# Order of the value transposes, the modulation sums and the softmaxes in the attention stages of a decoder trunk

## The chip, the core and the metric

One NeuronCore of one Trainium2 chip runs the whole program. The metric is the device time of one execution in microseconds (us). Engines are named as in the profile: PE is TensorE's matmuls and PEld its weight loads, DVE is VectorE, ACT is ScalarE, POOL is GpSimd, and SP is the engine whose queue issues most DMAs.

## The reference

One layer for a sequence of 512 positions of 1024 channels, in float32:

```python
cs = silu(c)
mod = cs @ w_ada + b_ada                  # 6 rows of 1024: shift1, scale1, gate1, shift2, scale2, gate2
h = rmsnorm(x, norm1_g) * (1 + scale1) + shift1
qa, ka, va, qd, kd, vd, ga, gd = split(h @ w_in)
out_a = sliding_window_attention(qa, ka, va, sinks)   # 8 heads, 2 kv heads, window 128, ALiBi, sinks
out_d = diff_attention(qd, kd, vd, lam)               # 4 heads, two softmax maps each, causal, ALiBi, RMSNorm
merged = sigmoid(ga) * (out_a @ w_branch_swa) + sigmoid(gd) * (out_d @ w_branch_diff)
x = x + gate1 * (merged @ w_out)
h2 = rmsnorm(x, norm2_g) * (1 + scale2) + shift2
x = x + gate2 * conv_ffn(h2)              # 1024 -> 2 x 2816, causal conv of width 3, GELU, -> 1024
return rmsnorm(x, final_g)
```

## The kernel before, in words

**Arithmetic.** A float32 product is made of three matmuls: each operand is split into a rounded part (`_h`, or `hi`) and a remainder (`_l`, or `lo`), and `mm3` adds hi·hi, hi·lo and lo·hi. A split is one ACT cast and one DVE subtraction (`split`, lines 115 and 116; `evac`, lines 430 to 434, for results that leave PSUM). So each weight block and each evacuated result costs both engines an instruction, DVE behind ACT.

**Stages.** The first 60 us normalise x and make the projections of the sliding-window queries, keys and values (tiles a0 to a5). Then come the projections of the differential heads together with the sliding-window attention (60 to 125 us), then the gates and branches of the first mixer together with the differential attention (125 to 230 us), then the gates of the second mixer, the merge and the output projection (to some 366 us), and the MLP. The change lies between 60 and 230 us.

**Who sets the order.** From line 485 on, TensorE's order is written by hand (`manual_schedule` for it alone): it executes what the program traces, in that order. DVE, ACT, POOL and SP are ordered by a planner when the kernel is built, by priority, then by the place in the trace, and by when the planner expects an operand to be ready; once built, each engine's queue is in order. `tc.high_priority(offset=HP)` puts instructions ahead of others that are ready. `tc.issue_after(ins)` queues what its block traces on the engine of `ins`, and only on that engine, behind `ins`; no wait for its end is added.

**Steps of filling.** `fill(n)` emits n steps of projection work on TensorE. A step is three matmuls of 512 columns; eight steps make a 128-column projection. `units` lists the projections to come, `prefetch` loads and splits their weights up to two ahead. A counter `tick` counts the steps. Work given to `after(n, fn)` is traced n steps later. At every eighth step, from step 8 on, `fill` calls `next(ada)`.

**Modulation rows.** `ada_rows` (line 750) makes four of the six modulation rows in eight halves of 512 columns. A call loads two blocks of w_ada (an SP DMA into a tile ra, one of four "raw" slots that weights share) and adds them, times silu(c), to the running sum `arow` with two DVE multiplies (lines 762 and 764). Behind the fourth call of a half the next one splits the sum (`arh`, `arl`) and hands the last part to `after(ADA_LAG, ...)`, with a lag of one step: `ada_spread` (line 771) sums over the partitions with two matmuls against ones, ACT copies a row out, and POOL writes it to `mod_rows` in DRAM. Past step 20 the multiplies have half the softmaxes' priority offset. The sum has one buffer, so the next half's first multiply waits for that DMA.

**Sliding-window attention.** Four pairs of heads. For a pair, `swa_scores(i, n0)` computes the scores of two 128-query blocks, with DVE adding the distance and taking the maximum (line 563); `swa_softmax(i)` scales the maxima (574), lets ACT do the exponentials with sums (575, 578) and DVE normalise (582, 583, 586), for the two heads j in turn; `swa_transpose(i, j)` transposes the probabilities of one head in two blocks (tile tp, line 598) into "t" banks of PSUM, of which there are two, and evacuates them into pTh and pTl; `swa_values(i)` multiplies them with the values `va`. `turn_va` (line 448) makes `va` out of the projected vaT by four transposes (tile pva, a "t" bank too) and two `evac`s. `evac_q(3)` evacuates the queries of the last pair, which share a bank with `swa_values`' result.

**Differential attention.** For head h and query block n, s = 4h + n: `diff_scores`, `diff_softmax` (lines 686 to 701: scaled maxima, two exponentials, then reciprocal, product with lambda, scaling and the difference of the two maps), `diff_transpose` (tile td, line 709) and, once a head is complete, `diff_values`. Blocks n = 0 and n = 1 of a head have their scores made together, and their softmaxes are traced one behind the other.

Of the kernel before, what the change touches and what calls it, by code (L numbers as in the profile page):

```python
# [11 lines left out]
ALU = mybir.AluOpType  # L12
# [15 lines left out]
HP = 100000  # L28
ST = 6
ADA_LAG = 1  # L30
# [6 lines left out]
SWA_FILL = (2, 2, 5, 2, 2, 2, 2, 3)  # L37
# [16 lines left out]
def kernel(  # L54
# [22 lines left out]
    nc = tc.nc  # L77
# [168 lines left out]
    ac, mods, wts = {}, {}, {}  # L246
# [191 lines left out]
    def evac_q(i):  # L438
        evac(qa[:, i, 0], qa[:, i, 1], acc6[i], qsc[:, i : i + 1])
# [55 lines left out]
    def fill(n):  # L495
        for _ in range(n):
            if not current:
                prefetch()
                if loaded:
                    wts, run = loaded.pop(0)  # L500
                    current.append(run(wts))
                    if tick[0]:
                        prefetch()
            if tick[0] == 7:
                prefetch()
            if current:
                try:
                    next(current[0])
                except StopIteration:
                    current.clear()  # L510
            for e in list(later):
                e[0] -= 1
                if e[0] <= 0:
                    later.remove(e)
                    e[1]()
            tick[0] += 1
            if tick[0] >= ADA_START and tick[0] % ADA_EVERY == 0:
                next(ada, None)

    def after(n, fn):  # L520
        later.append([n, fn])
# [14 lines left out]
    def swa_scores(i, n0):  # L536
        if n0 == 0:
            c = pairs[i] = Pair()
            c.mx, c.nm, c.lsum, c.es = (
                ap.tile([P, 2, NT], F32, tag=t, bufs=2, name=f"{t}{i}") for t in ("mx", "nm", "lsum", "es")  # L540
            )
            c.sb = [ap.tile([P, 2, P], F32, tag="st0", bufs=2, name=f"st{i}_0")]
            c.sb += [ap.tile([P, 2, 256], F32, tag="st", bufs=ST, name=f"st{i}_{n}") for n in range(1, NT)]
            c.pT = []
        c = pairs[i]
        sps = [sbank(f"sw{i}_{n0}_{j}", (P, 2, 256)) for j in range(2)]
        for n in (n0, n0 + 1):
            w = P if n == 0 else 2 * P
            k0 = max(0, n - 1) * P
            qs, ks = slice(n * P, (n + 1) * P), slice(k0, k0 + w)  # L550
            mm3_rows([
                (
                    sps[j][:, n - n0, :w],
                    [qa[64 * j : 64 * j + 64, i, b, qs] for b in range(2)],
                    [ka[64 * j : 64 * j + 64, b, ks] for b in range(2)],
                )
                for j in range(2)
            ])
        for n in (n0, n0 + 1):
            w = P if n == 0 else 2 * P  # L560
            for j in range(2):
                with tc.high_priority(offset=HP):
                    c.last = nc.vector.tensor_tensor_reduce(
                        c.sb[n][:, j, :w], sps[j][:, n - n0, :w], dsw[:, 256 - w : 256], 1.0, -3e38, ALU.add, ALU.max,
                        c.mx[:, j, n : n + 1],
                    )

    def swa_softmax(i):
        with tc.high_priority(offset=HP):
            c = pairs[i]  # L570
            for j in range(2):
                h = i + 4 * j
                slope = 2.0 ** -(h + 1)
                nc.vector.tensor_scalar(c.nm[:, j], c.mx[:, j], -slope, nsink[:, h : h + 1], ALU.mult, ALU.min)
                nc.scalar.activation(c.es[:, j], c.nm[:, j], AF.Exp, bias=sink[:, h : h + 1])
                for n in range(NT):
                    w = P if n == 0 else 2 * P
                    nc.scalar.activation(
                        c.sb[n][:, j, :w], c.sb[n][:, j, :w], AF.Exp, bias=c.nm[:, j, n : n + 1], scale=slope,
                        accum_out=c.lsum[:, j, n : n + 1],  # L580
                    )
                nc.vector.tensor_add(c.lsum[:, j], c.lsum[:, j], c.es[:, j])
                nc.vector.reciprocal(c.lsum[:, j], c.lsum[:, j])
                for n in range(NT):
                    w = P if n == 0 else 2 * P
                    nc.vector.tensor_scalar_mul(c.sb[n][:, j, :w], c.sb[n][:, j, :w], c.lsum[:, j, n : n + 1])

    def swa_transpose(i, j):
        c = pairs[i]
# [94 lines left out]
            scored[s] = mx, pm  # L684

    def diff_softmax(s):
        with tc.high_priority(offset=HP):
            h, n = divmod(s, NT)
            slope = 2.0 ** (-2 * (h + 1))
            mx, pm = scored[s]  # L690
            lsum = ap.tile([P, 2], F32, tag="dls", bufs=3, name=f"dls{h}_{n}")
            nc.vector.tensor_scalar_mul(mx, mx, -slope)  # L692
            for m in range(2):
                nc.scalar.activation(  # L694
                    pm[m], pm[m], AF.Exp, bias=mx[:, m : m + 1], scale=slope, accum_out=lsum[:, m : m + 1]
                )
            nc.vector.reciprocal(lsum, lsum)
            nc.vector.tensor_mul(lsum[:, 1:2], lsum[:, 1:2], nlam)
            nc.vector.tensor_scalar_mul(pm[1], pm[1], lsum[:, 1:2])
            nc.vector.scalar_tensor_tensor(pm[0], pm[0], lsum[:, 0:1], pm[1], ALU.mult, ALU.add)  # L700
            probs[s] = pm[0]

    def diff_transpose(s):
        h, n = divmod(s, NT)
# [45 lines left out]
    def ada_rows():  # L750
        for idx in range(4):
            for hf in range(2):
                c0 = (2 + idx) * D + hf * S
                ac = big.tile([P, S], F32, tag="sq2", name=f"arow{idx}{hf}")
                for k in range(0, KT, 2):
                    r = raw_tile([P, 2, S], f"ra{idx}{hf}_{k}")
                    nc.sync.dma_start(r, wada[k * P : (k + 2) * P, c0 : c0 + S].rearrange("(a p) n -> p a n", p=P))
                    with tc.high_priority(offset=HP // 2) if tick[0] > ADA_EASY else ExitStack():
                        for a in range(2):
                            cc = cs[:, k + a : k + a + 1]  # L760
                            if k + a == 0:
                                nc.vector.tensor_scalar_mul(ac, r[:, a], cc)
                            else:
                                nc.vector.scalar_tensor_tensor(ac, r[:, a], cc, ac, ALU.mult, ALU.add)  # L764
                    yield
                ah = big.tile([P, S], F32R, tag="g2b0", name=f"arh{idx}{hf}")
                al = big.tile([P, S], F32R, tag="g2b1", name=f"arl{idx}{hf}")
                split(ah, al, ac)
                after(ADA_LAG, lambda idx=idx, hf=hf, ac=ac, ah=ah, al=al: ada_spread(idx, hf, ac, ah, al))

    def ada_spread(idx, hf, ac, ah, al):
        pr = tbank(f"pr{idx}{hf}")
        nc.tensor.matmul(pr, onesr, ah, start=True, stop=False)
        nc.tensor.matmul(pr, onesr, al, start=False, stop=True)
        row = ac[0:1, :]
        nc.scalar.copy(row, pr[0:1, :])  # L776
        nc.gpsimd.dma_start(mod_rows[idx : idx + 1, hf * S : (hf + 1) * S], row)  # L777
# [27 lines left out]
        units.append((lambda: load_cols(win, COL_GA + j * P, f"wga{j}"), gate))  # L805
        units.append((load, branch))

    pairs, firsts, scored, probs, aTs = {}, {}, {}, {}, {}
    ada = ada_rows()
    add_head(0)  # L810
    add_head(1)
    fill(SWA_FILL[0])
    swa_scores(0, 0)
    with tc.issue_after(pairs[0].last.ins):
        fill(SWA_FILL[1])
        swa_scores(0, 2)
    with tc.issue_after(pairs[0].last.ins):
        swa_softmax(0)
        fill(1)
        evac_q(3)  # L820
        turn_va()
        fill(SWA_FILL[2] - 1)
    for i in range(SWA_PAIRS):
        more = i + 1 < SWA_PAIRS
        if more:
# [24 lines left out]
    for s in range(4 * DIFF_HEADS):  # L850
        h, n = divmod(s, NT)
        if n == 0 and 0 < h < 3:
            add_head(h + 1)
        elif s == 12:
            add_gate_a(2)
            add_gate_a(3)
        fill(DIFF_FILL[1])
        nxt = {0: (), 1: (s + 1,), 2: (s + 1,), 3: (s + 1, s + 2)}[n] if s < 15 else ()
        if nxt:
            diff_scores(*nxt)  # L860
        fill(DIFF_FILL[2])
        diff_transpose(s)
        for z in nxt:
            diff_softmax(z)
        if n == 0 and h:
            diff_values(h - 1)
            fill(DIFF_FILL[3])
    for j in range(4, KT):
        add_gate_a(j)
    fill(1)  # L870
# [602 lines left out]
    for i, (J, name) in enumerate(slots):  # L1473
# [21 lines left out]
        if i in rows_at:  # L1495
            hf = rows_at[i]
# [27 lines left out]
    e = cbuf[1][:, 1024:2048].rearrange("p (t n) -> p t n", n=S)  # L1524
# [269 lines left out]
```

## Time and profile before

| | |
|---|---|
| median of 3 runs | 715.82 us (714.96 to 717.16) |
| the profiled execution | 716.59 us |
| its span in the profile | 714.5 us |
| granted TensorE clock | 0.993 |
| busy: PE, PEld, DVE, ACT, POOL | 688.4, 603.0, 588.5, 384.2, 84.4 us |
| bytes moved by DMA | 121.82 MB, 170 GB/s on average |

The span runs from the first to the last instruction; the execution's own time is longer by what lies around it. The busy time of an engine is the sum over its instructions, with overlaps counted once. An entry such as `[2.09 <-DVE pTl L431]` behind an instruction says that its engine sat idle for 2.09 us before it and that the last thing it waited for was the instruction of line 431 on DVE that wrote pTl.

### The profile page before, as it was taken

How to read it: one execution, taken by the hardware profiler on the slowest of the kernel's cores; microseconds unless marked ns; L12 is line 12 of the kernel's file. 1: busy time of each engine (PE TensorE's matmuls, PEld its weight loads, DVE VectorE, ACT ScalarE, POOL GpSimd, SP SyncE). 2: the span in 40 equal slices, each digit the busy share in tenths (PEclk: the TensorE clock that was granted, in tenths of full speed). 3: DMA queues.
4: the chain of work that ended last, by engine and by line, in shares of the span. 5: the costliest groups of instructions: out<-in, count | busy, mean ns of one | idle time of the engine just before them, and what ended most of it. 6: DMA issues, size and time to landing. Idle time of an engine off the chain costs nothing. (4 is left out here: it accounts for less than half of the span.)

```text
span 714.5 us, 11275 instructions
## 1 busy us (share of the span) xinstructions
PE 688.4 (96%) x4187; PEld 603.0 (84%) x4187; DVE 588.5 (82%) x1125; ACT 384.2 (54%) x677; POOL 84.4 (12%) x101
## 2 busy tenths in 40 slices
PE   5999899999999999999999999999999999999994
PEld 5777778777787888888879999999999999888884
DVE  5998978797986774865479899888889899979996
ACT  3646566455554233432258666555555666656664
POOL 4000000001000100000012021111111102540300
PEclk9999999999999999999999999999999999999998
DMA  9983522453553664737717598877789738996903
GB/s 307 293 264 96 173 64 83 148 163 102 151 159 105 225 196 140 235 118 210 232 59 148 153 201 203 191 185 217 190 199 229 164 123 233 182 203 194 160 0 119
DMA packets 115863, 121.82 MB, mean 170 GB/s; under 512 B 4415, under 2 KB 93280, under 8 KB 115808
## 3 DMA queue, kind: packets, MB, share of 16 engines
q1 hardware_dynamic: 96894, 95.09, 42.1%
q0 software_dynamic: 18720, 25.73, 21.2%
q8 instruction: 33, 0.54, 0.3%
q10 hardware_dynamic: 194, 0.28, 0.1%
q14 instruction: 22, 0.18, 0.1%
HBM read 118.97 MB, written 2.11 MB: 169 GB/s over the span
## 5 line engine op out<-in xcount | busy, mean ns | idle before, releaser
L1133 PE MATMUL up<-t,m_whi 128*128 128x256 f32 x528 | 96.1, 283 | 0.0
L1133 PEld LDWEIGHTS up<-t,m_whi 128*128 128x128 f32 x528 | 82.3, 192 | 0.0
L1133 PE MATMUL up<-t,m_wlo 128*128 128x256 f32 x264 | 74.7, 283 | 0.1
L1133 PE MATMUL up<-bh,p_wlo 128*128 128x256 f32 x232 | 65.7, 284 | 0.6 <-DVE p_wlo L1076 0.6
L1133 PE MATMUL up<-bh,p_whi 128*128 128x256 f32 x232 | 65.6, 283 | 0.0
L1133 PE MATMUL up<-bl,p_whi 128*128 128x256 f32 x232 | 65.6, 283 | 0.0
L1133 PEld LDWEIGHTS up<-t,m_wlo 128*128 128x128 f32 x264 | 50.6, 192 | 0.3 <-DVE m_wlo L1076 0.3
L1133 PEld LDWEIGHTS up<-bh,p_wlo 128*128 128x128 f32 x232 | 44.4, 192 | 1.1 <-DVE p_wlo L1076 1.1
L1133 PEld LDWEIGHTS up<-bh,p_whi 128*128 128x128 f32 x232 | 44.5, 192 | 0.0
L1133 PEld LDWEIGHTS up<-bl,p_whi 128*128 128x128 f32 x232 | 44.5, 192 | 0.0
L1044 POOL DMA_DIRECT2D s<-in_w_up_dram x21 | 27.2, 1385 | 143.0 <-DMA s<-in_w_up_dram 92.7
L764 DVE SCALAR_TENSOR_TENSOR arow<-ra,cs,arow 128x512 f32<-128x512 f32 x56 | 41.9, 748 | 1.4 <-DMA ra<-in_w_ada_dram 0.7
L1076 DVE TENSOR_TENSOR m_wlo<-s,m_whi 128x1024 fp32r<-128x1024 f32 x31 | 37.7, 1216 | 2.0 <-ACT m_whi L1072 2.0
L1072 ACT CAST m_whi<-s 128x1024 fp32r<-128x1024 f32 x31 | 32.5, 1047 | 9.3 <-DVE s L1066 5.9
L1133 PE MATMUL up<-t,p_whi 128*128 128x256 f32 x176 | 32.2, 283 | 0.0
L175 POOL TENSOR_TENSOR r<-ms,mhalf 128x1 f32<-128x1 f32 (+1 forms) x16 | 13.4, 838 | 144.7 <-DVE ms L173 77.2
L694 ACT ACTIVATE sd<-sd,dmx 128x128 f32<-128x128 f32 (+3 forms) x32 | 17.8, 556 | 22.0 <-DVE dmx L692 15.4
L777 POOL DMA_DIRECT2D mod_rows<-arow x8 | 4.3, 540 | 200.5 <-ACT arow L776 200.3
L1133 PEld LDWEIGHTS up<-t,p_whi 128*128 128x128 f32 x176 | 27.4, 192 | 0.2 <-issue 0.2
L1140 ACT ACTIVATE gT<-a,cv 128x512 f32<-128x512 f32 x22 | 17.7, 813 | 17.6 <-DVE a L1175 17.3
L1072 ACT CAST p_whi<-wa 128x1024 fp32r<-128x1024 f32 x18 | 18.7, 1042 | 12.0 <-PE up L1133 10.8
L1133 PE MATMUL up<-t,p_wlo 128*128 128x256 f32 x88 | 24.9, 283 | 0.0
(485 smaller groups left out, 2119.5 us busy)
## 6 DMA issues: line engine op xcount, KB each, us to landing
ra<-in_w_ada_dram SPq DMA_DIRECT2D x32, 512.0 KB, 4.2
wa<-in_w_up_dram SPq DMA_DIRECT2D x22, 512.0 KB, 4.6
s<-in_w_up_dram SPq DMA_DIRECT2D x21, 512.0 KB, 5.0
s<-in_w_up_dram POOLq DMA_DIRECT2D x21, 512.0 KB, 6.5
adaw<-in_w_ada_dram SPq DMA_DIRECT2D x16, 512.0 KB, 5.1
w<-in_w_in_dram SPq DMA_DIRECT2D x12, 512.0 KB, 3.9
a<-in_w_up_dram SPq DMA_DIRECT2D x11, 512.0 KB, 4.7
b<-in_w_down_dram SPq DMA_DIRECT2D x10, 512.0 KB, 3.9
```

Source lines behind the costliest of these rows:

```text
L175: nc.gpsimd.tensor_tensor(r0, ms, mhalf[:, :n], ALU.pow)
L694: nc.scalar.activation(pm[m], pm[m], AF.Exp, bias=mx[:, m : m + 1], scale=slope, accum_out=lsum[:, m : m + 1])
L764: nc.vector.scalar_tensor_tensor(ac, r[:, a], cc, ac, ALU.mult, ALU.add)
L777: nc.gpsimd.dma_start(mod_rows[idx : idx + 1, hf * S : (hf + 1) * S], row)
L1044: nc.gpsimd.dma_start(dst, upblock(*blk), accum_op=ALU.add)
L1072: nc.scalar.copy(W[J, name][0], R[J, SRC[name]])
L1076: nc.vector.tensor_sub(lo, R[J, SRC[name]], hi.bitcast(F32))
L1133: nc.tensor.matmul(o[u], w[:, k, cu], b[:, k], start=name in ("p1", "m5", "p2") and k == 0 and x == 0, stop=k == 3 and x == 2, skip_group_ ...
L1140: nc.scalar.activation(grow(j), av[J][:, u], AF.Identity, bias=cv[:, 66 + j : 67 + j], scale=cv[:, 44 + j : 45 + j])
```

## The change

Three things are moved; the arithmetic is the same.

1. `turn_va` is traced between the first and the second scores of pair 0 instead of behind them. `evac_q(3)` and the steps behind the first softmax are also queued on ACT behind that softmax's last exponential.
2. From the first softmax to the end of the differential attention a modulation call that falls due is counted (`due`) and not made. `ada_due(end)` makes all that are due, traced behind a softmax and with their DVE instructions queued behind its last one: each sliding-window softmax, and each differential one but those of n = 0. In that stretch the spread follows 9 steps behind the split instead of 1.
3. The softmax of block n = 1 is queued behind that of n = 0, on ACT behind its last exponential and on DVE behind its last instruction.

```diff
@@ fill
             if tick[0] >= ADA_START and tick[0] % ADA_EVERY == 0:
+                due[0] += 1
+                if not hold[0]:
+                    ada_due()
+
+    due, hold = [0], [False]
+
+    def ada_due(behind=None):
+        with tc.issue_after(behind.ins) if behind else ExitStack():
+            while due[0]:
+                due[0] -= 1
                 next(ada, None)
@@ swa_softmax
-                    nc.scalar.activation(
+                    c.exp = nc.scalar.activation(
...
-                    nc.vector.tensor_scalar_mul(c.sb[n][:, j, :w], c.sb[n][:, j, :w], c.lsum[:, j, n : n + 1])
+                    end = nc.vector.tensor_scalar_mul(c.sb[n][:, j, :w], c.sb[n][:, j, :w], c.lsum[:, j, n : n + 1])
+        ada_due(end)
@@ diff_softmax
-        with tc.high_priority(offset=HP):
+        with tc.high_priority(offset=HP), ExitStack() as order:
             h, n = divmod(s, NT)
+            if n == 1:
+                for e in ends[s - 1]:
+                    order.enter_context(tc.issue_after(e.ins))
...
-                nc.scalar.activation(
+                exp = nc.scalar.activation(
...
-            nc.vector.scalar_tensor_tensor(pm[0], pm[0], lsum[:, 0:1], pm[1], ALU.mult, ALU.add)
+            end = nc.vector.scalar_tensor_tensor(pm[0], pm[0], lsum[:, 0:1], pm[1], ALU.mult, ALU.add)
+            ends[s] = exp, end
             probs[s] = pm[0]
+        if n:
+            ada_due(end)
@@ ada_rows
-                after(ADA_LAG, lambda ...: ada_spread(idx, hf, ac, ah, al))
+                after(ADA_LAG if not hold[0] else 9, lambda ...: ada_spread(idx, hf, ac, ah, al))
@@ the order around the first pair
     with tc.issue_after(pairs[0].last.ins):
-        fill(SWA_FILL[1])
+        fill(1)
+        turn_va()
+        fill(SWA_FILL[1] - 1)
         swa_scores(0, 2)
+    hold[0] = True
     with tc.issue_after(pairs[0].last.ins):
         swa_softmax(0)
-        fill(1)
-        evac_q(3)
-        turn_va()
-        fill(SWA_FILL[2] - 1)
+        with tc.issue_after(pairs[0].exp.ins):
+            fill(1)
+            evac_q(3)
+            fill(SWA_FILL[2] - 1)
@@ behind the differential attention's loop
+    hold[0] = False
     for j in range(4, KT):
         add_gate_a(j)
```

More of the change, by code (lines that the diff above doesn't have):

```diff
@@ L768, in ada_rows @@
                 split(ah, al, ac)
-                after(ADA_LAG, lambda idx=idx, hf=hf, ac=ac, ah=ah, al=al: ada_spread(idx, hf, ac, ah, al))
+                after(ADA_LAG if not hold[0] else 9, lambda idx=idx, hf=hf, ac=ac, ah=ah, al=al: ada_spread(idx, hf, ac, ah, al))
     def ada_spread(idx, hf, ac, ah, al):
@@ L806, in add_gate_a @@
         units.append((load, branch))
-    pairs, firsts, scored, probs, aTs = {}, {}, {}, {}, {}
+    pairs, firsts, scored, probs, aTs, ends = {}, {}, {}, {}, {}, {}
     ada = ada_rows()
```

## The prediction

> **What bounds the kernel now.** The page came first: its engine totals and its PE slices say that TensorE works nearly all the time.
>
> ```profile
> PE 688.4 (96%) x4187; PEld 603.0 (84%) x4187; DVE 588.5 (82%) x1125; ACT 384.2 (54%) x677; POOL 84.4 (12%) x101
> PE   5999899999999999999999999999999999999994
> ```
>
> Then busy time by stage, for the stretch that the change touches (heads' projections and both attentions, 60 to 230 us) and the stretch behind it. The columns are: length, PE, PEld, DVE, ACT, POOL, clock, DMA share, GB/s.
>
> ```profile
> 60.00:80.00 20.00, 17.91 (x116) 13.84 (x115) 17.32 (x60) 10.25 (x30) 0.00 (x0) 1.00 0.35 107
> 80.00:125.00 45.00, 44.19 (x291) 37.41 (x289) 37.65 (x112) 28.91 (x82) 0.70 (x1) 1.00 0.34 100
> 125.00:230.00 105.00, 102.70 (x548) 81.09 (x547) 86.40 (x234) 53.52 (x123) 6.06 (x6) 1.00 0.48 141
> 230.00:366.00 136.00, 136.00 (x606) 112.32 (x605) 86.19 (x113) 46.68 (x63) 7.62 (x12) 1.00 0.59 182
> ```
>
> TensorE idles 2.09 + 0.81 + 2.30 = 5.20 us in the touched stretch and never in the 136 us behind it, at full clock. Its order is written by hand, so a microsecond of idle removed there moves everything behind it by a microsecond; 5.20 us is all there is to gain. The waits of PE from 60 to 366 us say whom it waits for (total, times, longest):
>
> ```profile
> PE tp L598 <- DVE pTl L431: 2.9, 2, 2.1
> PE td L709 <- DVE sd L700: 1.8, 4, 1.1
> PE od L120 <- DVE aTl L431: 0.5, 1, 0.5
> ```
>
> All three are VectorE, so DVE's order decides. The two timelines show the largest places, first PE, then DVE (start, duration):
>
> ```profile
> 74.76 0.55 PE L598 MATMUL tp<-ident,st 128*128 128x128 f32 x3 [2.09 <-DVE pTl L431]
> ...
> 91.68 1.01 PE L598 MATMUL tp<-ident,st 128*128 128x128 f32 x7 [0.81 <-DVE pTl L431]
> ...
> 153.11 0.30 PE L709 MATMUL td<-ident,sd 128*128 128x128 f32 x1 [1.10 <-DVE sd L700]
> ```
>
> ```profile
> 74.01 0.69 DVE L431 TENSOR_TENSOR pTl<-tp,pTh 128x512 fp32r<-128x512 f32 x1
> 74.62 0.42 DVE L431 TENSOR_TENSOR va<-pva,va 128x256 fp32r<-128x256 f32 x1
> ...
> 90.33 0.69 DVE L116 TENSOR_TENSOR arl<-arow,arh 128x512 fp32r<-128x512 f32 x1
> 90.94 1.15 DVE L431 TENSOR_TENSOR pTl<-tp,pTh 128x512 fp32r<-128x512 f32 x2
> ...
> 151.43 0.75 DVE L764 SCALAR_TENSOR_TENSOR arow<-ra,cs,arow 128x512 f32<-128x512 f32 x1
> ```
>
> At 74 us both "t" banks are full: one holds the transposed values pva until 75.04, the other the first probability blocks until 74.70. At 91 the split of a modulation row (arl) stands ahead of the evacuation that frees the bank. At 148 to 152 three modulation multiplies stand inside the softmax that TensorE waits for.
>
> **Part 1: values transposed earlier.** turn_va moves from behind the second scores to between the two; its four transposes take 0.35 us (66.38 to 66.73) and are neither added nor removed. The second scores come 0.35 us later, so do their maxima and exponentials. vaT has been ready since 61.62 and ACT idles from 62.2 to 67.07, so the two casts and two subtractions fall into idle time (DVE idles 64.38 to 65.68), and the bank is free by some 66.3. Both transposes of the first half then run on end, 72.06 to 72.96, and 2.09 us go.
>
> What is late next: two fill steps of 0.70 us follow, so the second half's transposes come at 74.4 and need those same two banks. The exponentials end at 71.9 (71.55 + 0.35). Now evac_q(3) and two weight casts, which ACT did at 61.50, 56.85 and 72.20, are queued behind the last exponential. With only the q cast first (0.70) the hi casts run 72.6 to 73.5; DVE, through with the second half's scaling at 73.3, subtracts to 74.0 and 74.5: no wait. One weight cast first (1.03) makes it 75.3, a wait of 0.5; both, 1.5. I take 0.4, as the transposes' evacuations have high priority and the weight casts none. Part 1 saves 1.7, bounds 0.6 to 2.1. On DVE evac_q(3)'s subtraction (0.74) and one weight subtraction (1.22) leave 67 to 69.5 for 73 on; 1.23 us of modulation work leaves 69.6 to 70.9 in exchange. q3's bank is wanted at 81.2, the weight (v of head 0) at 80.5: cover of 5 us or more. If ACT or DVE used it up, each 1.03 or 1.22 us cast or subtraction would show on PE in full.
>
> **Part 2: modulation sums behind the softmaxes.** The 64 multiplies and 8 splits stay (0.67 us from start to start). Up to the last attention step, a sum that falls due waits for the next softmax's last DVE instruction. Its DMAs (SP), the splits' casts (ACT) and the POOL write follow it in trace order; only the DVE instructions get the edge. Due at step 8: behind softmax 1; 16 and 24: softmax 2; 32: softmax 3; 40 and 48: the second differential softmax. So the split at 90.33 leaves the swa stage. The evacuation at 90.94 can start at 90.33: saves 0.6 of 0.81, bounds 0 to 0.81.
>
> At 153.11 the first block's softmax loses the three multiplies (2.0 us), by order alone: from its maxima (148.6) two exponentials (to 149.8 with the cast ahead of them), then about 1.2 us of DVE as at 130.10 to 131.17, ends at 151.0, and TensorE is there at 152.0. Saves 1.0, bounds 0 to 1.1.
>
> The four waits left are 0.17 (172.84), 0.24 (197.62), 0.33 (221.81) and 0.46 (224.07). Ahead of 221.81 a multiply (216.71) and a split cast (217.49) precede the exponentials; these go. The first two have no sum in front and stay; behind the last stands a weight subtraction (222.20, 1.22). I take 0.5, bounds 0 to 1.2.
>
> The price: behind swa softmax 2 come four multiplies (2.7 us) near 100 to 104, where none were. The first bank for the transposes at 105.99 is freed at about 105.9, so there is no slack: one multiply ahead costs 0.67. I take 0.4, bounds 0 to 1.5 (twice 0.67, rounded up). The spread of a row comes 9 steps (6.3 us) after the split instead of 1; its two in-order matmuls wait for the split's subtraction only if DVE needs longer than that, and 2 multiplies, cast and subtraction are 1.3 + 0.6 + 0.7 = 2.6. The final row is finished at 301, the merge stage ends at 366: the end has 65 us of cover.
>
> **Part 3: second block behind the first.** With n = 1 scaling of the maxima, exponentials and the rest queue behind the first block's. From 131.1: 0.16, two exponentials 1.0, then 1.2 of DVE: 133.5 instead of 132.83. Its transposes come at 137.80, and in the other heads 8 us or more after the softmax. Costs 0; if the cover went, 0.7 a head, 2.8 in all, as part of the last rival.
>
> **Sum.** 1.7 + 0.6 + 1.0 + 0.5 - 0.4 = 3.4 us. The profiled execution took 716.59 (span 714.5 and 2.09 around it), so 713.2; it lay 0.77 above the median 715.82 of the three runs, so the time is 712.4. All bounds good: 5.2, 710.6. All bad: 0.6 - 1.5 = -0.9, 716.7.
>
> **A rule weighed.** The row: in 60 to 230 us PE idles 5.2 us, while PEld is busy 132.3 of 170 us. The Trainium skill (Perfetto Trace Analysis, Identifying the Most-Contended Engine) holds matmul busy time for a poor gauge and would judge by weight loading. By that the headroom would be 22%, not 3%, and the transposes' stalls would be the PEld row's 4.1 us, not 2.9: a sum of 4.6. I keep PE: outside the stalls matmuls of 512 columns start every 0.23 us with a load of 0.19 in each, a pace that this change does not touch.
>
> **Rivals.**
> *The stalls move* (715.0, a chance of 0.23). Two "t" banks and a DVE that was 14.9 of 15.0 us busy from 80 to 95 remain; what leaves one place stands ahead of the next evacuation. For it: zero slack at 105.99, and the casts put off behind the exponentials. Part 1 then nets 0.6, the rest 1.0, minus 0.8: 715.82 - 0.8. Against: DVE idles 24% from 95 to 125, where most sums go. The Trainium skill (Perfetto Trace Analysis, Optimization Strategy) reads a gap that repeats as too few buffers; the trace shows the gap at two of the four pairs, not at all, so order has a part. To this rival also belongs that the planner gives the freed bank no earlier use: then the 2.09 stays.
>
> *Weight loads queue behind rows that hold raw slots* (719.0, 0.20 with its kin). Weights and modulation rows share four raw slots and SP's in-order queue:
>
> ```profile
> SPq L477 <- DVE arow L764: 12.2, 6, 5.4
> ```
>
> So weight loads already wait for these multiplies. With the spread 8 steps later (5.6 us) and sums issued two at a time, four rows can fill all slots until the spread's copy is out. Place: v of head 2, split by 156.0 and wanted at 164.96, 9.0 us of cover. The rival decides when one load is held over 9 us longer: two of those waits each longer by 5.6 hold it 11.2, a stall of 2.2 in each of three heads, 6.6 against 3.4 saved, 3.2 worse: 715.82 + 3.2. Against: two rows loaded by 84.6 sat in slots until 120.28 with no PE wait at all.
>
> **Chances.** The forecast has 0.57. Within 0.3% (2.15 us, about what a measurement of this kernel tells from no change) means 713.67 to 717.97. Of the forecast a small part falls above 713.67 and of the first rival a small part below: faster 0.55, same 0.25, slower 0.20. The range reaches from all bounds good to just past the bound of slower: 710.6 to 718.0; the slower cases beyond it are under 2 in 10.
>
> **What would show it.** Right: no PE wait near 72 to 75, pva's subtractions before 66.5, arl absent from 80 to 125, the fifth differential softmax free of arow, td waits at 0.6 or less. Wrong: tp waits of over 1.5 us in all, or PE waiting for w_l, w_h, arl or a DMA from 60 to 230. The sum fails if 230 to 366 gets idle PE time.

## The result and the profile after

The changed kernel takes 728.88 us (median of 4 executions, 726.79 to 729.84) against 715.95 (4 executions): 1.0172 times as long, 95% interval 1.0152 to 1.0193. It is 12.9 us slower, where 3.4 us less were forecast, and 10.9 above the range. The profiled execution took 729.35 us.

From the page of the changed kernel, busy time and the PE slices:

```profile
PE 694.6 (95%) x4187; PEld 606.0 (83%) x4187; DVE 588.9 (81%) x1125; ACT 384.7 (53%) x677; POOL 84.2 (12%) x101
PE   5999999989999899999999999999999999999995
```

As many instructions as before, and DVE is as busy: no work was added, PE only idles more. The 9th slice (145 to 164 us) and the 14th (236 to 255) lost their full digits. Busy time by stage, with the columns of the table before (the last window ends where the merge stage now ends):

```profile
60.00:80.00 20.00, 19.18 (x122) 14.61 (x120) 15.51 (x60) 12.19 (x34) 0.00 (x0) 1.00 0.20 64
80.00:125.00 45.00, 42.61 (x279) 35.84 (x279) 35.48 (x107) 27.05 (x80) 0.00 (x0) 1.00 0.34 100
125.00:230.00 105.00, 97.94 (x518) 76.07 (x516) 81.24 (x226) 51.66 (x120) 5.93 (x6) 1.00 0.41 121
230.00:379.00 149.00, 145.58 (x638) 119.41 (x639) 96.73 (x128) 51.03 (x70) 8.21 (x13) 0.98 0.61 187
```

The first 20 us do gain (idle 0.82, not 2.09). The other three windows lose: 2.39, 7.06 and 3.42 us of idle where 0.81, 2.30 and 0 stood. The waits of PE from 58 to 300 us of the changed kernel (total, times, longest; the transposes' lines are now L609 and L726, the softmax's last step L714):

```profile
PE td L726 <- DVE sd L714: 3.5, 4, 1.4
PE tp L609 <- DVE pTl L431: 2.4, 3, 1.2
PE pr L790 <- ACT arh L115: 1.8, 1, 1.8
PE pq L121 <- DVE w_l L116: 1.5, 1, 1.5
PE pr L791 <- DVE arl L116: 1.2, 2, 0.7
PE td L726 <- DVE dmx L706: 1.2, 1, 1.2
PE pw L119 <- DVE qkv L434: 0.8, 1, 0.8
PE pq L119 <- ACT w_h L115: 0.6, 1, 0.6
PE od L120 <- DVE aTl L431: 0.4, 1, 0.4
PE sd L126 <- DVE qkv L431: 0.2, 1, 0.2
```

These add up to 13.6 us; the three lines of before gave 5.2. Two kinds are new, weights (w_h, w_l: 2.1) and row spreads (pr: 3.0), and there is more of the softmax (td 4.7 instead of 1.8). No one kind carries the loss. Their places in PE's timeline:

```profile
75.90 1.01 PE L609 MATMUL tp<-ident,st 128*128 128x128 f32 x7 [0.82 <-DVE pTl L431]
...
153.43 0.50 PE L121 MATMUL pq<-hThA,w_l 128*128 128x512 f32 x1 [1.50 <-DVE w_l L116]
...
178.49 0.63 PE L726 MATMUL td<-ident,sd 128*128 128x128 f32 x4 [1.40 <-DVE sd L714]
...
244.69 0.80 PE L790 MATMUL pr<-arh,onesr 128*128 128x512 f32 x1 [1.82 <-ACT arh L115]
```

The wait at 244 costs twice: the granted clock falls with it. Two windows (the clock is the third number from the end):

```profile
244.00:246.00 2.00, 0.80 (x1) 0.29 (x1) 1.85 (x3) 0.64 (x2) 0.26 (x1) 0.60 0.79 210
246.00:250.00 4.00, 3.97 (x9) 3.14 (x10) 1.55 (x5) 0.58 (x1) 1.65 (x3) 0.50 0.50 147
```

At 0.50 a matmul starts every 0.43 us instead of 0.23. The clock averages 0.89 from 230 to 260, which is 3.3 us, a little of it while PE stood idle anyway. From the first scores (62.20 before, 62.97 after) to the MLP's first product (374.10 and 386.95) the kernel became 12.1 us longer. In this stretch the kernel before idles 6.5 us, as it also has a wait of 1.34 us at 369.06, just ahead of the MLP, that the changed kernel lacks. So 7.1 us of idle and some 3 of clock give 10 of the 12.1; the other 2 are not traced to a row here. The new waits lie from 80 to 247 us, and the clock is a consequence of one of them.

SP's queue shows what moved. Four loads of modulation rows and, behind them, the three loads of head 2's weights, before:

```profile
117.55 7.97 SPq L757 DMA_DIRECT2D ra<-in_w_ada_dram  x4
126.73 8.23 SPq L477 DMA_DIRECT2D w<-in_w_in_dram  x3
```

and after:

```profile
126.05 16.93 SPq L774 DMA_DIRECT2D ra<-in_w_ada_dram  x4
...
146.27 7.50 SPq L477 DMA_DIRECT2D w<-in_w_in_dram  x3
```

The weights come 19.5 us later, and ACT then stands idle for the first of them, ahead of the two waits for w_h and w_l:

```profile
150.10 1.05 ACT L115 CAST w_h<-w 128x1024 fp32r<-128x1024 f32 x1 [1.58 <-DMA w<-in_w_in_dram]
```

This looked like the second rival of the prediction, and the experiments began with it.

### The profile page after: what moved, and what is told of

Same layout as the page of the kernel before. It is cut to its first block, busy times and chain, and to the rows that moved or that the text cites. A ratio compares the mean times of both kernels' runs of the same rounds, so it can differ in the third digit from the quotient of the medians.

```text
span 727.4 us, 11252 instructions
## 1 busy us (share of the span) xinstructions
PE 694.6 (95%) x4187; PEld 606.0 (83%) x4187; DVE 588.9 (81%) x1125; ACT 384.7 (53%) x677; POOL 84.2 (12%) x101
## 3 DMA queue, kind: packets, MB, share of 16 engines
HBM read 118.97 MB, written 2.11 MB: 166 GB/s over the span
## 5 line engine op out<-in xcount | busy, mean ns | idle before, releaser
L1093 ACT CAST p_whi<-wa 128x1024 fp32r<-128x1024 f32 x18 | 18.7, 1040 | 12.1 <-PE up L1154 9.0
```

Of the source, the lines that this page charges most:

```text
L1093: nc.scalar.copy(W[J, name][0], R[J, SRC[name]])
```

## The experiments

Theory A: late spreads keep the row sum and the raw slots occupied, weight loads queue behind them and reach PE too late. The first eight runs set it against theory B: VectorE's order by itself, sums in a bunch and softmaxes in series. Theory C, formed after these: what is shifted are VectorE's multiplies for the rows, which then stand in front of the softmax steps that PE waits for. Theory D, set against C at the end: not the multiplies in particular, but any long work on VectorE in this stage. They do not exclude one another. The runs stand by subject, not in the order of time.

**The three parts alone.** The first part alone (`turn_va` moved, the fills queued behind the exponentials):

> The kernel before with the first part alone: values transposed between the first two scores, and evac_q(3) and the steps behind the first softmax queued on ACT behind its last exponential. In the changed kernel the wait of 2.09 us at the second block of the first transposes is gone, but 0.82 us (next transposes, for pTl) and 0.81 us (v projection, for the evacuation of pq) stand in its place. Both theories agree: 0 to 1 us faster than before, a ratio of 0.998 to 1.001, with these two waits in the profile and no wait for a weight.

717.25 us (10 executions), ratio 1.0023, interval 1.0007 to 1.0040. The transposes' wait fell from 2.9 to 0.6, more than counted, but PE then waits at a place that the prediction had covered by "5 us or more":

```profile
80.91 0.47 PE L119 MATMUL pw<-hThA,w_h 128*128 128x512 f32 x1 [3.10 <-DVE qkv L434]
```

pw needs the bank of pq, the queries of the first differential head. DVE's part of that evacuation runs only at 80.08 (74.95 before), behind a row multiply and a weight subtraction:

```profile
78.28 0.75 DVE L764 SCALAR_TENSOR_TENSOR arow<-ra,cs,arow 128x512 f32<-128x512 f32 x1
78.94 1.22 DVE L116 TENSOR_TENSOR w_l<-w,w_h 128x1024 fp32r<-128x1024 f32 x1
80.08 0.69 DVE L434 SCALAR_TENSOR_TENSOR qkv<-pq,qkv 128x512 fp32r<-128x512 f32 x1
```

ACT had cast it at 72.96. The wait also costs clock, which is 0.50 from 82 to 84 us and 0.83 on average from 80 to 90. That is 1.7 us, as much as the whole part costs.

The third part alone (the second block's softmax behind the first's):

> The kernel before with the third part alone: the n = 1 softmax of each differential head behind the n = 0 one. Theory A (late weights: the slowdown comes from modulation rows that hold raw slots, so that weight loads queue behind them on SP) expects no loss: the wait of 1.10 us at the fifth transposes shrinks or stays, ratio 0.997 to 1.001. Theory B (VectorE's order: the sums in a bunch behind the softmaxes and the softmaxes in series make TensorE wait by themselves) expects some of the loss here: 1 to 4 us slower, ratio 1.002 to 1.006, with waits of PE for sd or dmx at the n = 0 and n = 1 transposes.

718.69 us (10), ratio 1.0034, interval 1.0017 to 1.0051. DVE in the fifth softmax, where the other block's steps can no longer run in between (L700 to L703 are the first block's last four steps):

```profile
149.86 0.15 DVE L700 RECIPROCAL dls<-dls 128x2 f32<-128x2 f32 x1
149.93 0.73 DVE L768 SCALAR_TENSOR_TENSOR arow<-ra,cs,arow 128x512 f32<-128x512 f32 x1
150.58 0.15 DVE L701 TENSOR_TENSOR dls<-dls,nlam 128x1 f32<-128x1 f32 x1
150.65 1.22 DVE L116 TENSOR_TENSOR w_l<-w,w_h 128x1024 fp32r<-128x1024 f32 x1
151.79 0.28 DVE L702 TENSOR_SCALAR sd<-sd,dls 128x128 f32<-128x128 f32 x1
151.98 0.74 DVE L768 SCALAR_TENSOR_TENSOR arow<-ra,cs,arow 128x512 f32<-128x512 f32 x1
152.65 0.34 DVE L703 SCALAR_TENSOR_TENSOR sd<-sd,dls,sd 128x128 f32<-128x128 f32 x1
```

Between four steps of 0.92 us lie 2.69 us of other work, and PE waits 1.95 us at 153.13 (1.10 before). The second part alone (row sums behind softmaxes, lag 9):

> The kernel before with the second part alone: modulation calls counted and made behind softmaxes, spread 9 steps behind the split. Theory A expects nearly the whole loss here: 8 to 13 us slower (ratio 1.011 to 1.018), the first spread near 134 us instead of 115, the weight loads of head 2 issued after 140 instead of 127, PE waits for w_h, w_l, arh or arl. Theory B expects 4 to 8 us slower (1.006 to 1.011), the rest being with the softmaxes in series, and PE waits for sd, not for weights.

726.85 us (4), ratio 1.0165, interval 1.0129 to 1.0200. So the second part is most of the loss. The size is theory A's (8 to 13), not B's (4 to 8); PE's waits are mixed, 3.5 us for the softmax's last step, 2.2 for weights and 1.5 for spreads. Over one baseline the three ratios give +1.6, +2.4 and +11.8 us, 15.8 together, against 12.3 by the ratio of the whole: some 3.5 us of the parts overlap.

**Inside the second part.** It has two edits: the sums wait for a softmax, and the spread comes 9 steps behind the split. The changed kernel with a lag of 1 throughout (`ADA_LAG if not hold[0] else 9` becomes `ADA_LAG`):

> The changed kernel with the spread one step behind the split throughout, instead of 9 in the held stretch. The spread then comes 8 steps (5.6 us) sooner at every half row. Theory A: the raw slots are freed some 5 us sooner, so the weights come some 5 us sooner and 3 to 7 us of the 12.9 come back (719 to 726), unless TensorE now waits at each spread for the split itself, queued behind a softmax: that would show as PE waits for arl or arh at each of the held spreads, 1 to 3 us each. Theory B: no gain, or slower, 728 to 735.

744.57 us (4), ratio 1.0406, interval 1.0372 to 1.0440: worse by another 16. PE's waits:

```profile
PE pr L791 <- DVE arl L116: 14.1, 4, 6.7
PE pr L790 <- ACT arh L115: 3.9, 2, 2.4
```

With the split queued behind a softmax, a spread traced one step later makes PE, in its written order, stand still for that softmax. The lag of 9 is needed if the sums are held. Its own price is seen the other way round, in the kernel before with nothing but the lag:

```diff
-                after(ADA_LAG, lambda ...: ada_spread(idx, hf, ac, ah, al))
+                after(ADA_LAG if not 9 < tick[0] < 170 else 9, lambda ...: ada_spread(idx, hf, ac, ah, al))
```

> The kernel before with only the lag changed: from step 10 to step 169 a row is spread 9 steps behind its split instead of 1; sums are made when due, not behind softmaxes. The spreads come 5.6 us later, so the raw slots of the next half's first rows are held 5.6 us longer. Theory A: head 2's loads go from 127 to about 132 us, which its 13 us of cover mostly bear: 0 to 3 us slower (ratio 1.000 to 1.004). Theory B expects no change (0.999 to 1.001).

728.84 us (4), ratio 1.0194, interval 1.0173 to 1.0215: this line alone costs as much as the whole change. Neither theory had expected more than 3 us. And there is no wait for a weight or a spread; PE waits for the softmax:

```profile
PE td L709 <- DVE sd L700: 9.1, 5, 2.7
PE tp L598 <- DVE pTl L431: 2.9, 2, 2.1
```

One of the five, PE and then DVE:

```profile
137.20 0.30 PE L709 MATMUL td<-ident,sd 128*128 128x128 f32 x1 [2.06 <-DVE sd L700]
```

```profile
134.60 0.16 DVE L697 RECIPROCAL dls<-dls 128x2 f32<-128x2 f32 x1
134.72 0.75 DVE L764 SCALAR_TENSOR_TENSOR arow<-ra,cs,arow 128x512 f32<-128x512 f32 x1
135.39 0.16 DVE L697 RECIPROCAL dls<-dls 128x2 f32<-128x2 f32 x1
135.46 0.14 DVE L698 TENSOR_TENSOR dls<-dls,nlam 128x1 f32<-128x1 f32 x1
135.52 0.75 DVE L764 SCALAR_TENSOR_TENSOR arow<-ra,cs,arow 128x512 f32<-128x512 f32 x1
136.18 0.15 DVE L698 TENSOR_TENSOR dls<-dls,nlam 128x1 f32<-128x1 f32 x1
136.25 0.54 DVE L699 TENSOR_SCALAR sd<-sd,dls 128x128 f32<-128x128 f32 x2
136.71 0.74 DVE L700 SCALAR_TENSOR_TENSOR sd<-sd,dls,sd 128x128 f32<-128x128 f32 x2
```

Before, the second row half was started at 120.28 and its multiplies lay between the two attentions. Here its first multiply is at 130.31, and they lie among the steps of the first two differential softmaxes. That first multiply does harm already by waiting for the one buffer of the sum:

```profile
130.31 0.49 DVE L762 TENSOR_SCALAR arow<-ra,cs 128x512 f32<-128x512 f32 x1 [4.00 <-DMA mod_rows<-arow]
```

DVE stands idle for 4.00 us until the row before is written out, although PE has the scores ready at 128.32 (its matmuls run from 127.36). The instructions that take their maxima start at 131.97, 4.6 us after the scores' start, instead of 2.8 in the kernel before (127.88 after 125.04). So two things delay this softmax: the blocked queue, then the multiplies between its steps. The Trainium skill (TensorE: Matmul & The Clock Gate, Architectural detail) calls the queues of ACT and DVE strictly first in, first out; this case agrees, as the product at 135.46 ran behind the multiply of 134.72, although the reciprocal of its block had ended at 134.76. An order that was fixed when the kernel was built cannot step round a multiply, nor round one that waits.

The waits are not the whole price. From the first scores to the MLP's first product (62.98 to 386.77) this run is 11.9 us longer than the kernel before, of which 7.0 are idle. Three times the clock falls to about 0.5, behind the waits at 75.56, 137.20 and 234.46, some 1.7 us each. The first of these waits, 2.12 us, stands in the kernel before too, 2.09 us long and without a fall.

How the loss grows with the lag, first with the lag of 9 for the first half's spread alone (`ADA_LAG if idx or hf else 9`), then with 4 steps for all spreads of the stretch:

> The kernel before with a lag of nine steps for the first half row's spread alone; every other spread keeps its lag of one, and most of VectorE's order stays as it was. Theory C (each late spread moves its own half's multiplies into the softmaxes): about one of six spreads between 60 and 260, so 1 to 4 us slower than before, 717 to 720. Theory A (the first late spread holds the slots ahead of head 2's weights, and all the loss follows from there): 8 to 13 us slower, 724 to 729, with head 2's first weight load issued after 130.

> The kernel before with a lag of four steps in place of nine between steps 10 and 170. Loss in proportion to the lag (three extra steps of eight): 3 to 7 us slower, 719 to 723. Theory C, a matter of where the multiplies fall: no proportion, anything from 0 to 13 slower, told apart by a wait of td on the scores' last softmax step in the stretches in which the multiplies lie between softmax steps. Theory A: near 0 to 4, as the first spread would come only some 7 us later, still ahead of head 2's need.

718.60 us (5), ratio 1.0055, interval 1.0032 to 1.0079; and 721.64 (4), ratio 1.0092, interval 1.0065 to 1.0118. One spread costs 2.7 us by the medians (theory C's 1 to 4), though head 2's loads start at 133.24; a lag of four steps, three of the eight extra ones, costs some 5.7 us, not far from proportion (5.0 of 13.3). The td waits are 5.6 and 6.6 us. Theory A's step, all loss out of the first late spread, is not there.

**Are the late weights the cause?** A second buffer for every second row half lets its multiplies start before the first half is written out. For lack of room the buffer `of` of the differential attention went from two to one. In the changed kernel, then in the kernel before:

```diff
-        of = ap.tile([P, S], F32, tag="of", bufs=2, name=f"of{h}")
+        of = ap.tile([P, S], F32, tag="of", bufs=1, name=f"of{h}")
...
-                ac = big.tile([P, S], F32, tag="sq2", name=f"arow{idx}{hf}")
+                if hf and idx < 2:
+                    ac = ap.tile([P, S], F32, tag="arow2", name=f"arow{idx}{hf}")
+                else:
+                    ac = big.tile([P, S], F32, tag="sq2", name=f"arow{idx}{hf}")
```

> The changed kernel with a second buffer for the running sum: the second halves of the first two modulation rows go to a buffer of their own (its 2 KB per partition come from the second buffer of the differential heads' normalised output), so that their multiplies need not wait for the spread of the half before. Rows then leave their raw slots at once and the weight loads behind them come early again. Theory A (late weights): the loads of head 2's weights are issued before 132 us instead of 146, PE waits for w_h and w_l vanish, and 5 to 9 of the 12.9 us come back (720 to 724). Theory B (VectorE's order by itself): the sums stand behind the softmaxes as before, so 727 to 730.

> The kernel before with the same second buffer, as the control of the run ahead of it. The weight loads were early enough there, so both theories expect within 2 us of before: the bunch of multiplies at 147 to 157 moves forward, which may take the 1.10 us wait at 153 away (714 to 717), and one buffer less for the normalised output may cost something.

728.28 us (4), ratio 1.0181, interval 1.0165 to 1.0197: nothing won, head 2's loads stayed at 144.89 and the wait for w_l grew to 4.4 us, so the first run doesn't decide about late weights. The second does: its loads come at 120.06, 6.7 us earlier than in the kernel before, and it takes 726.37 us (4), ratio 1.0136, interval 1.0103 to 1.0169, with td waits of 4.6, tp of 4.0 and od of 1.9 us. Early weights alone do not make it fast. (Both theories had expected it within 2 us of before. How much of its loss the single `of` buffer costs was not separated.)

Releasing the sums that are due ahead of the second differential scores (`ada_due()` before `diff_scores(0, 1)`), so that the first split is early:

> The changed kernel with the two calls that are due at the end of the sliding-window stage made there, ahead of the first differential scores, and not behind the second differential softmax. The first split is then early, but its spread still comes 9 steps behind step 53, near 133 us, and the raw slots are held until then. Theory A: the wait for arl at the first spread (0.70 us) goes, the late weights stay: 0.5 to 2 us faster than the changed kernel (727 to 728.4). Theory B: the same or faster by up to 4, as one bunch of sums leaves the softmaxes.

727.97 us (4), ratio 1.0176, interval 1.0161 to 1.0191. The first spread's wait for arl went, as expected, and 0.9 us with it: within what a measurement tells from nothing.

**Taking work off VectorE.** If the place in DVE's queue is the cause, shorter instructions in it should give the time back, with the spreads as many steps behind as ever. The multiplies then cover 64 of 512 columns, and the modulation rows lack the rest of their sum.

```diff
-                                nc.vector.scalar_tensor_tensor(ac, r[:, a], cc, ac, ALU.mult, ALU.add)
+                                nc.vector.scalar_tensor_tensor(ac[:, :64], r[:, a, :64], cc, ac[:, :64], ALU.mult, ALU.add)
```

In the kernel before, in the changed one, and in the one with the lag alone:

> Control for the next run. The kernel before with each accumulating multiply of the row sums over 64 of its 512 columns (the other columns of the modulation rows then lack seven eighths of their sum; loads, slots, splits and spreads stay). About 27 us of VectorE work between 60 and 260 us goes. Theory C (the multiplies stand in front of softmax steps on VectorE): the kernel before has few such collisions, so only 1 to 5 us faster than 715.9, 711 to 715. Theory A (the rows' slots are held too long and head 2's weights come late): before, they come in time, so no gain, 714 to 717.

> The changed kernel with the same thin multiplies (same part left out). Theory C: most of the 13 us disappears; this stands at most 4 us over the thin kernel before, and the td waits of 3.5 + 1.2 us fall below 2. Theory A: slots and loads are tied to the held spreads as before, so the difference to the thin kernel before stays at 9 to 13 us and the loads of head 2's weights are still issued after 140.

> The kernel before with the lag of nine steps and the thin multiplies (64 of 512 columns; the modulation rows lack seven eighths of their sum). Theory C (row multiplies in front of softmax steps): the 13 us of the lag shrink as those of the changed kernel did, to at most 4 us over the thin kernel before (717.0), so 716 to 721, td waits on the last softmax step below 3 instead of 9.1. Against it (the lag costs by late spreads or late loads, not by VectorE): 726 to 730.

Before: 717.00 us (10), ratio 1.0022, interval 1.0008 to 1.0036. Some 20 us less of DVE work (42 multiplies of 0.28 instead of 0.75 us between 60 and 260) bring nothing, where theory C had expected a gain of 1 to 5 us. The waits moved to other tiles (va 1.7, qkv 0.9), and the clock fell once (0.54 from 170 to 172 us), which may hide a gain of up to 1.7 us. Changed: 719.43 (4), ratio 1.0062, interval 1.0042 to 1.0081, 2.4 above that control instead of 12.9. Its waits on the softmax's last step and its queue for head 2's weights:

```profile
PE td L726 <- DVE sd L714: 0.5, 1, 0.5
```

```profile
142.70 7.96 SPq L477 DMA_DIRECT2D w<-in_w_in_dram  x3
```

The loads come 3.6 us earlier than in the changed kernel, still 16 later than before, and no wait for a weight is left. So this run doesn't price late loads by themselves: in the changed kernel they do cost part of the 2.1 us, and the cast ahead of arh at 244 waited for a load too. Theory A falls as the whole account because the lag alone costs as much without one wait for a weight.

Nor does the run hold DVE's order fixed, as the planner orders shorter instructions anew. In the changed kernel two multiplies (140.77 and 141.84) lie between a reciprocal at 140.69 and its scaling at 142.50; in the thin one all three stand ahead of the reciprocal (they start at 139.60, it at 140.48, the scaling at 140.87). Length and place changed together.

With the lag alone: 723.70 (4), ratio 1.0108, interval 1.0081 to 1.0136, 6.7 above the control instead of 13. The td waits on sd fell from 9.1 to 2.5 as theory C says, but the time missed its 716 to 721. Beside them seven waits remain (va 1.7, dmx 1.4, ta 1.3, aTh 1.1 and less). About half of the lag's cost is thus in the multiplies. A part of the other half that shorter multiplies cannot touch is in the trace: DVE again stands idle, 4.15 us until 128.19, behind the first multiply that waits for the row's write, and PE waits at 133.64 and 142.44. What that is worth in time was not separated.

Whether it must be the row multiplies: the changed kernel with another load cut, the weights' subtractions over 16 of 128 columns.

```diff
+        if len(shape) == 3 and shape[2] == P and 9 < tick[0] < 170:
+            nc.gpsimd.memset(lo.bitcast(F32), 0.0)
+            nc.scalar.copy(hi, raw)
+            nc.vector.tensor_sub(lo[:, :, :16], raw[:, :, :16], hi[:, :, :16].bitcast(F32))
+        else:
+            split(hi, lo, raw)
```

> The changed kernel with another of VectorE's loads cut by about as much: the subtractions that split the heads' and gates' weights (1.22 us each, 18 of them between 60 and 260 us) over 16 of 128 columns, the rest of the low part set to zero on GpSimd (the low parts of those weights are then mostly left out of the sums). If VectorE is simply too full in this stage (theory D), any 20 us taken off it give the loss back: 717 to 721. If it is the row multiplies in the places that the late spreads give them (theory C), most of it stays: 724 to 730. In between: both.

719.66 us (7), ratio 1.0068, interval 1.0042 to 1.0093. Fourteen of the eighteen subtractions took 0.29 instead of 1.22 us, 13 us in all, and 9.2 us came back by the medians, 7.4 by the ratios, with the multiplies at full size and head 2's loads at 143.71. (A shorter subtraction also serves the matmul that waits for w_l sooner, but those waits had been 1.5 us only.) So it is theory D: not this one instruction, but anything long that stands in front of a step PE is waiting for. Weight subtractions do it as well as multiplies, as the 150.65 above already showed. VectorE is not simply too full: from 125 to 230 us it is busy 81.2 us in the changed kernel and was busy 86.4 before.

**A better version.** The first part without the queueing behind the exponentials, and nothing else:

```diff
-        fill(SWA_FILL[1])
+        fill(1)
+        turn_va()
+        fill(SWA_FILL[1] - 1)
...
         evac_q(3)
-        turn_va()
```

> A candidate better than both: the kernel before with v turned between the first two sets of scores, but without the fills queued behind the first softmax's exponentials, and with no other part. If the wait of 3.1 us for pq's evacuation that the first part alone showed came from that queueing, it goes and the saved tp waits stay: 713 to 715. If it came from v's turn itself: 716 to 718.

713.54 us (12), ratio 0.9971, interval 0.9957 to 0.9985: the only kernel here whose interval lies below that of the kernel before, by 0.3%. PE's waits of the swa stage:

```profile
74.44 1.01 PE L598 MATMUL tp<-ident,st 128*128 128x128 f32 x7 [1.00 <-DVE pTl L431]
89.85 1.01 PE L598 MATMUL tp<-ident,st 128*128 128x128 f32 x7 [0.96 <-DVE pTl L431]
```

The 2.09 us before the second transposes are 1.00, the wait for pq does not occur. So the kernel gains 2.3 us by the medians, and queueing evac_q(3) and the fills behind the exponentials costs 3.7 (717.25 - 713.54). In the trace only 0.9 us of the gain lies at the transposes (2.90 of waits became 1.96). Another 1.3 is the wait at 369.06, far behind, which this run lacks; whether the turn takes it away was not tested.

## Why the prediction was wrong

Its reading of what bounds the kernel held: PE's written order, with DVE's order deciding. That a microsecond of idle there "moves everything behind it by a microsecond" held with the other sign.

*Part 1: saves 1.7.* The mechanism was right: the bank is free early, and in the part alone the transposes wait 0.6 us instead of 2.9. The step that failed is the cover: "q3's bank is wanted at 81.2 ... cover of 5 us or more". Its list of what is put off, evac_q(3) and two weight casts, lacked the evacuation of pq, whose bank is wanted at 77.8; that came 3.10 us too late, and the clock fell behind it. With both the part alone cost 1.6 instead of saving 1.7. In the full change the same wait was 0.81.

*Part 2: 0.6 + 1.0 + 0.5 - 0.4.* The gains are real: no arl near 91, and the wait at 153 is 0.29 at 150.01. The price behind the second softmax was 1.20 us at 106.77, inside the bounds of 0 to 1.5. The failed step is the sentence "The spread of a row comes 9 steps (6.3 us) after the split instead of 1; its two in-order matmuls wait for the split's subtraction only if DVE needs longer than that". It asked who waits for the spread, and not what waits behind it: the single row sum, and so the next half's eight multiplies, splits and loads, all shifted into the softmaxes, with DVE blocked for 4.00 us ahead of the first. Costed at nothing, it is 13 us by itself, 7 of them idle and most of the rest clock. Even the question that was asked had the wrong answer: 3.0 us of waits for pr, 1.82 of them where the cast arh ran at 244.02 behind that of a weight that had landed late, at 243.07.

*Part 3: costs 0, 2.8 if the cover goes.* Alone it cost 2.4. The place was not the cover that it looked at; a serial chain of short DVE steps leaves gaps that the planner fills with long instructions, which the two interleaved blocks had filled for each other.

*Rivals.* The second named the right edge (a late spread that holds slots) and the right head, at 0.20 and 6.6 us. Its price was read from the wrong queue: SP's loads did become late, yet PE waited only 2.1 us for weights in all. The first, stalls that move, was priced as a few instructions near 105.99, not as the reordering of the whole stage. The signs of being wrong came true: tp waits of 2.4 us, PE waiting for w_l, w_h and arl. So did "the sum fails if 230 to 366 gets idle PE time": 3.42 us from 230 to 379, and with it the fall of the clock, which no case had.

*The weighed rules.* Judging by PEld would have read the result no better: PEld is busy 606.0 us instead of 603.0 while the time grew by 12.9. The rule of too few buffers for a gap that repeats (the Trainium skill, Perfetto Trace Analysis, Optimization Strategy) found no support: a second row buffer, with one `of` buffer less, changed nothing after the change and cost 10.8 us before it.

*What stays open.* Half of what the lag alone costs, 6.7 us, remains with thin multiplies; the blocked queue is in that trace, but no run took it away by itself. And in the changed kernel the shares of softmax steps, weights and spreads are read from its trace, not set apart by runs.

## What to carry to other kernels

When an edit delays the last reader of a single-buffered tile, follow the buffer, not the reader: list everything that starts when it comes free, and look at which critical chains that work will now stand in front of in its engines' queues. Cover measured at the operand's consumer does not bound that cost. A DVE that is busy four fifths of the time has room on average, but a chain of 0.15 us steps is delayed by 0.7 to 1.2 us for each long instruction that the plan drops between two of them, and by up to 4 us where one of these itself waits for the buffer; an order that avoids this by luck is part of the kernel's speed, and moving one spread by a few steps can lose it.

## What the runs showed of the hardware

Two waits of PE, 1.82 and 0.54 us long with one matmul between them, brought the granted clock from 1.00 to 0.50 (0.60 in 244 to 246 us, 0.50 to 250, 0.69 in 250 to 252). The Trainium skill (TensorE: Matmul & The Clock Gate, Part 1: The HAM clock gate) states half rate after an idle window of about 3.4 us that runs freely. The value of 0.50 agrees; here no single idle stretch was as long as that window. Counted as time at half rate, these windows give 6.8 us. In the run of the first part, behind a wait of 3.10 us, the count is 3.4 (0.85, 0.50 and 0.80 in three windows of 2 us from 80 to 86), a loss of 1.7 us.

The length of a wait does not tell whether the clock falls. At the first transposes a wait of 2.09 us in the kernel before and one of 2.12 in the run of the third part left it at 1.00; one of 2.12 us with the lag alone and one of 2.11 with four steps brought it to 0.50 and 0.51. With lag and thin multiplies a wait of 1.42 us at 142.44 was enough (0.50 from 144 to 146). So a wait of 1.4 to 3 us can cost its own length and another 1.7 us, and two runs that idle alike can differ by that.
